# Hybrid attention and pooling layer: softmax division moved from the values' product to the split of the exponentials

## The chip, the cores and the metric

The kernel runs on one core of one Trainium2 chip. The metric is device time in microseconds (us), measured for whole executions; lower is better. One execution was also taken with the hardware profiler, and all rows below come from that one.

## The reference

One decoder layer over 1024 tokens of width 1024. A normalised input is projected to six pieces by one matrix; four of them go through causal average pooling or through attention over a sliding window of 128 tokens (8 heads of 64, 2 key/value heads, a position bias and a sink value for each head); both results are gated, projected out and added to the input.

```python
h = rmsnorm(x, norm_pre)
pool_u, pool_gate, q, k, v, attn_gate = split(h @ w_in)
pool_out = pool_mixer(pool_u, pool_w, pool_scale) * silu(pool_gate)
# attention, for each block of 128 queries, over its own and the previous block of keys
scores = q @ k.T * HEAD_DIM ** -0.5 + bias
probs = softmax(concat([scores, sink]))[..., :-1]
attn_out = (probs @ v) * silu(attn_gate)
y = concat([pool_out, attn_out]) @ w_out
x = x + rmsnorm(y, norm_post)
```

What matters here is `probs`: an exponential divided by the sum of its row, one sum for each query and head.

## The kernel before

All matrix products run in half precision, with each operand split into a high and a low part of 16 bits; three products (high by high, high by low, low by high) make up one of full precision. ScalarE writes a high part (a scaled copy), VectorE the low part (what the copy lost).

The program is written in one order by hand, and each engine executes its own instructions in that order. After a prologue, the body is a loop over **slots** `s` from 5 to 33: a slot is the projection of one group of 128 output columns for one half of the tokens (`proj`, 24 matmuls of 128x512 into the tile `acc`, of which there are two, so that a slot can start only when the result of the slot two before it has been read out by `land_slot`). At half a slot, `proj` calls `middle()`, which puts small matmuls between the two groups of 12: `spread` (the tile of that name, a transposition by which the largest weight is found; `amall`, `wp`, `ws`, `wu` on VectorE and the split of the next weights `whl` follow from it) and, late in the loop, the pooling products (`mixed`).

Attention is woven into these slots, two for each block `n` of 128 queries, an even one (s = 5 + 2n) and an odd one (s = 6 + 2n). Even slot: `score_mm(n)` on TensorE, `score_land(n)` on VectorE (bias, mask, row maximum `negm`), `exps(n)` on ScalarE: eight exponentials, one for each head, that also give the eight sums `sums`. Odd slot: `turn(n)` on ScalarE (high part of the exponentials, tile `ph`), `turn_low(n)` on VectorE (low part), then a DMA transposes `ph` into `full`. Next even slot: `mask(n)` on GpSimd makes two masked copies (`own`, `full`). Next odd slot: `pv_mm(n)` on TensorE multiplies by the values, into the one tile of `ps_pv`.

The division by the sums comes at the end of this. `turn_low` takes the reciprocals and has GpSimd spread them over a tile `r` of 128x512; `divide(n)`, called in `middle()` of the next even slot, has TensorE transpose `r` in four matmuls into the tile `rb`, which shares its place in PSUM with the values' product `pvo`, and ScalarE reads `rb` out into `cat`. Later `pv_land(n)` on VectorE multiplies the values' product by what `divide` left in `cat`.

Where pooling starts (slots 18 to 25), `land_u` on ScalarE writes the strip `ug` (and its end, `tails`), `pool_windows` on VectorE turns it into `res` one slot later, and `pool_mm` on TensorE uses `res` one slot after that. In slots 20 to 23 ScalarE also applies Silu to one quarter of the gates in `cat`, for which it loads another table once.

Of the kernel before, what the change touches and what calls it, by code (L numbers as in the profile page):

```python
# [9 lines left out]
F32 = mybir.dt.float32  # L10
# [3 lines left out]
AF = mybir.ActivationFunctionType  # L14
ALU = mybir.AluOpType
# [4 lines left out]
P = 128  # L20
# [3 lines left out]
NB = S // P  # L24
HD = 64
# [10 lines left out]
def trunk(ctx: ExitStack, tc, x, w_in, pool_w, pool_scale, attn_sinks, w_out, norm_pre, norm_post, out):  # L36
    nc = tc.nc
# [10 lines left out]
    t2 = ctx.enter_context(tc.tile_pool(name="t2", bufs=8))  # L48
# [4 lines left out]
    ps_pv = ctx.enter_context(tc.tile_pool(name="ps_pv", bufs=1, space=PSUM))  # L53
# [11 lines left out]
    def block_of(n):  # L65
        return slice(n * P, (n + 1) * P)
# [88 lines left out]
    ident = const.tile([P, P], F32, name="ident")  # L155
# [5 lines left out]
    cat = big.tile([P, KT, S], F32, name="cat")  # L161
# [59 lines left out]
    def low_w(ch):  # L221
        w, s = whl[ch], halves.pop(ch)
        nc.vector.scalar_tensor_tensor(  # L223
            w[:, 1], raws.pop(ch), s, w[:, 0], op0=ALU.mult, op1=ALU.subtract
        )
# [78 lines left out]
    vo = const.tile([P, 1], F32, name="vo")  # L304
# [41 lines left out]
    att_sc, att_s, att_p, att_f, att_r, att_o = {}, {}, {}, {}, {}, {}  # L346
# [3 lines left out]
    def score_mm(n):  # L350
        k0 = 0 if n else 1
        for pr in range(2):
            banks = [bank("sc").rearrange("p (c b s) -> p c b s", c=2, b=2) for _ in range(2)]
            for ci in range(2):
                for i, (a, b) in enumerate(PASSES):
                    for kv in range(2):
                        rows = slice(kv * HD, (kv + 1) * HD)
                        nc.tensor.matmul(  # L358
                            banks[kv][:, ci, k0:, :],
                            qT[rows, a, 2 * pr + ci, block_of(n)],  # L360
                            kT[rows, b, (n - 1 + k0) * P : (n + 1) * P],
                            start=i == 0, stop=i == 2,
                        )
            att_sc[n, pr] = banks
# [29 lines left out]
    def turn(n):  # L394
        st, sums = att_s.pop(n)
        ph = att.tile([P, 2, 8, P], F16, tag="ph", name="ph")
        nc.scalar.activation(ph[:, 0], st[:, :, :P], AF.Copy, scale=4096.0)  # L397
        att_f[n] = (st, sums, ph)

    def turn_low(n):  # L400
        st, sums, ph = att_f[n]
        nc.vector.scalar_tensor_tensor(  # L402
            ph[:, 1], st[:, :, :P], 4096.0, ph[:, 0], op0=ALU.mult, op1=ALU.subtract
        )
        full = att.tile([P, 2, 8, P], F16, tag="full", name="full", bufs=2)
        nc.sync.dma_start_transpose(
            full.rearrange("p a j t -> p (a j) t"), ph.rearrange("p a j s -> p (a j s)")
        )
        nc.vector.reciprocal(sums, sums)  # L409
        r = t2.tile([P, 512], F32, tag="t2", name="r")  # L410
        nc.gpsimd.tensor_copy(  # L411
            r.rearrange("p (c kv d) -> p c kv d", c=4, kv=2),
            sums.rearrange("p (kv c) -> p c kv", kv=2).unsqueeze(3).broadcast_to([P, 4, 2, HD]),
        )
        att_f[n] = full
        att_r[n] = r

    def mask(n):
        full = att_f.pop(n)
        if n == 0:  # L420
            att_p[n] = [(0, full)]
            return
        own = att.tile([P, 2, 8, P], F16, tag="own", name="own")
        f, o = (t.rearrange("p a j t -> p (a j) t") for t in (full, own))
        nc.gpsimd.affine_select(  # L425
            o, f, pattern=[[0, 16], [1, P]], compare_op=ALU.is_ge, fill=0.0,
            base=0, channel_multiplier=-1,
        )
        nc.gpsimd.affine_select(  # L429
            f, f, pattern=[[0, 16], [-1, P]], compare_op=ALU.is_ge, fill=0.0,  # L430
            base=-1, channel_multiplier=1,
        )
        att_p[n] = [(n, own), (n - 1, full)]


    def divide(n):
        r = att_r.pop(n)
        rb = ps_pv.tile([P, 512], F32, tag="pv", name="rb")
        for c in range(4):
            nc.tensor.transpose(rb[:, block_of(c)], r[:, block_of(c)], ident)  # L440
        nc.scalar.activation(
            cat[:, 4:8, block_of(n)], rb.rearrange("p (c t) -> p c t", t=P), AF.Copy, scale=vo
        )

    def pv_mm(n):
        parts = att_p.pop(n)
        pv = ps_pv.tile([P, 512], F32, tag="pv", name="pvo")
        total = 3 * len(parts)
        i = 0
        for tt, t in parts:  # L450
            for a, b in PASSES:
                for kv in range(2):
                    nc.tensor.matmul(  # L453
                        pv[kv * HD : (kv + 1) * HD, :],
                        vst[:, a, tt, kv * HD : (kv + 1) * HD], t[:, b, 4 * kv : 4 * kv + 4, :],
                        start=i == 0, stop=i == total - 1,
                    )
                i += 1
        att_o[n] = pv

    def pv_land(n):
        dst, pv = cat[:, 4:8, block_of(n)], att_o.pop(n)
        nc.vector.tensor_tensor(dst, pv.rearrange("p (c t) -> p c t", t=P), dst, op=ALU.mult)


    tails = const.tile([P, 4, PAD], F32, name="tails")
# [176 lines left out]
    with tc.manual_schedule(engines={ENG.PE, ENG.Activation, ENG.DVE, ENG.Pool, ENG.SP}):  # L643
# [136 lines left out]
        for s in range(5, last):  # L780
            ch, half = slots[s]
            n, odd = (s - 5) // 2, (s - 5) % 2
            if not odd:
                if 2 <= n <= NB + 1:
                    pv_land(n - 2)
                if 1 <= n <= NB:
                    mask(n - 1)
                if n < NB:
                    score_mm(n)
            elif n < NB:  # L790
                turn(n)
            if 20 <= s < 24:
                gate = cat[:, s - 20, :]
                nc.scalar.activation(gate, gate, AF.Silu)
            gates = list(pool_out)
            for key in list(pool_in):
                pool_windows(*key)

            for c2 in list(halves):
                low_w(c2)  # L800
                load_next()
            for _ in range((1, 1, 1, 0, 0, 2, 2, 2, 2, 2, 2)[s - 23] if s >= 23 else 0):
                if wo_lo < wo_hi:
                    low_wo(wo_lo)
                    wo_lo += 1


            def middle():
                for key in list(bounds):
                    if key[0] in ("wo", "c"):  # L810
                        spreads[key] = spread(bounds.pop(key))
                        if key[0] == "c":
                            scale_cat(key[1])
                        else:
                            pow2_of(widest(spreads.pop(key)), wop, wos, 14)
                            state["wo"] = True
                    elif first_slot[key] == s + 3:
                        spread_w((key,))
                        scale_w((key,))
                        high_w(key)  # L820
                if not odd and 1 <= n <= NB:
                    divide(n - 1)
                for key in gates:
                    pool_mm(*key)

            acc = proj(ch, half, middle)
            if odd and 1 <= n <= NB:
                pv_mm(n - 1)
            if odd and n < NB:
                turn_low(n)  # L830

            for c2 in order:
                if first_slot[c2] == s + 5:
                    bound_w(c2)

            if 9 <= s < 9 + KT:
                wo_raw["b", s - 9] = load_wo(s - 9)
            if 11 <= s < 11 + KT:
                bound_wo(s - 11)
            if s == 11 + KT:  # L840
                m = bounds["wo", 0] = col("wom")
                nc.vector.tensor_reduce(m, wom, axis=AX.X, op=ALU.max)
            if s >= 30:
                bound_cat(s - 30)
            if s >= 23 and wo_hi < KT:
                split_wo(wo_hi)
                wo_hi += 1
            if not odd and n < NB:
                score_land(n)
            for key in gates:  # L850
                pool_gate(*key)
            land_slot(ch, half, acc)
            if not odd and n < NB:
                exps(n)
            if s == 5 + 2 * NB + 1:
                open_late()
            if 21 <= s < 21 + KT:
                wo_raw["o", s - 21] = load_wo(s - 21)
            if s >= last - 2:
                load_res(s - last + 2)  # L860
# [47 lines left out]
```

## Time and profile before

| | |
|---|---|
| median of three executions | 346.24 us (345.97 to 347.31) |
| the profiled execution | 346.77 us, of which 345.1 us lie between its first and last instruction |
| TensorE, matmuls | 323.6 us busy, 94% of the span |
| VectorE | 199.1 us, 58% |
| ScalarE | 168.9 us, 49% |
| GpSimd | 66.2 us, 19% |
| granted TensorE clock, mean | 0.989 of full speed |

The shares are means over the whole span. A busy share says which engine has most work; whether a stretch is set by that engine is seen from the timeline, by who waits for whom there. In rows, PE is TensorE, DVE is VectorE, ACT is ScalarE, POOL is GpSimd, and L with a number is a line of the kernel before.

### The profile page before, as it was taken

How to read it: one execution, taken by the hardware profiler on the slowest of the kernel's cores; microseconds unless marked ns; L12 is line 12 of the kernel's file. 1: busy time of each engine (PE TensorE's matmuls, PEld its weight loads, DVE VectorE, ACT ScalarE, POOL GpSimd, SP SyncE). 2: the span in 40 equal slices, each digit the busy share in tenths (PEclk: the TensorE clock that was granted, in tenths of full speed). 3: DMA queues.
4: the chain of work that ended last, by engine and by line, in shares of the span. 5: the costliest groups of instructions: out<-in, count | busy, mean ns of one | idle time of the engine just before them, and what ended most of it. 6: DMA issues, size and time to landing. Idle time of an engine off the chain costs nothing.

```text
span 345.1 us, 5054 instructions
## 1 busy us (share of the span) xinstructions
PE 323.6 (94%) x1913; PEld 166.4 (48%) x1913; DVE 199.1 (58%) x423; ACT 168.9 (49%) x368; POOL 66.2 (19%) x73
## 2 busy tenths in 40 slices
PE   4689999999999999999979998799999999999993
PEld 2588556545444445445434443344444444444442
DVE  4976771537697445796979567793563633410222
ACT  4966831275656685878484443354463433211011
POOL 1100303000132344050423000000000333212330
PEclk9969999999999999999999999999999999999999
DMA  7986240001437367395240892010000241233111
GB/s 280 255 230 159 86 123 0 2 19 44 122 122 208 120 164 179 66 181 126 62 122 0 291 245 76 0 63 0 0 2 0 68 150 59 90 123 122 61 63 61
DMA packets 52090, 35.73 MB, mean 104 GB/s; under 512 B 35041, under 2 KB 45793, under 8 KB 52066
## 3 DMA queue, kind: packets, MB, share of 16 engines
q1 hardware_dynamic: 52064, 35.40, 37.1%
q8 instruction: 15, 0.25, 0.3%
q14 instruction: 9, 0.07, 0.1%
q10 hardware_dynamic: 2, 0.00, 0.0%
HBM read 27.01 MB, written 4.19 MB: 90 GB/s over the span
## 4 chain that ended last, share of the span: by engine, by line
PE 46%; DVE 19%; issue 16%; ACT 9%; POOL 6%; DMA 2%; POOLq 0%; DVEq 0%; SPq 0%; ACTq 0%
PE acc L290 30%; POOL o L639 5%; ACT st L387 4%; PE pv L272 3%; PE y L272 3%; DVE whl L223 3%; DVE st L375 2%; PE tp L250 2%; DVE win L489 2%; PE acc L272 2%; PE sc L358 2%; DVE sc L374 2%; DVE o L636 2%; PE pvo L453 1%; DVE negm L380 1%
## 5 line engine op out<-in xcount | busy, mean ns | idle before, releaser
L290 PE MATMUL acc<-hT,whl 128*128 128x512 f16 x792 | 176.7, 379 | 1.1 <-ACT gt L529 1.1
L290 PEld LDWEIGHTS <-whl 128*128 128x128 f16 x792 | 76.6, 98 | 93.9 <-issue 8.3
L272 PE MATMUL y<-wo,chl 128*128 128x512 f16 (+2 forms) x408 | 83.6, 366 | 0.0
L272 PEld LDWEIGHTS <-chl 128*128 128x128 f16 x408 | 39.0, 98 | 43.5
L219 ACT ACTIVATE whl<-wraw,ws 128x1024 f16<-128x1024 f32 x18 | 20.4, 1148 | 34.6 <-DVE wu L213 22.4
L609 ACT ACTIVATE junk<-y 128x512 bf16<-128x512 f32 (+2 forms) x17 | 9.7, 572 | 54.9 <-PE y L272 54.9
L387 ACT ACTIVATE st<-st,negm 128x129 f32<-128x129 f32 x64 | 24.8, 390 | 12.6 <-DVE negm L380 9.6
L611 DVE SCALAR_TENSOR_TENSOR eps_of<-yss,eps_of 128x1 f32<-128x1 f32 x17 | 3.2, 185 | 45.9 <-ACT junk L609 45.9
L631 POOL TENSOR_TENSOR yf<-eps_of,mhalf 128x1 f32<-128x1 f32 x7 | 3.9, 551 | 119.2 <-DVE eps_of L611 119.2
L223 DVE SCALAR_TENSOR_TENSOR whl<-wraw,ws,whl 128x1024 f16<-128x1024 f32 x18 | 23.7, 1327 | 0.0
L402 DVE SCALAR_TENSOR_TENSOR ph<-st,ph 128x1024 f16<-128x1024 f32 x8 | 9.8, 1226 | 21.6 <-ACT ph L397 21.6
L91 ACT ACTIVATE whl<-wraw 128x1024 bf16<-128x1024 f32 x18 | 18.8, 1049 | 1.5 <-DMA wraw<-in_w_in_dram 1.5
L639 POOL TENSOR_TENSOR o<-o,xr 128x512 f32<-128x512 f32 x14 | 17.5, 1269 | 9.1 <-DVE o L636 9.1
L425 POOL TENSOR_SCALAR_AFFINE_SELECT own<-full 128x2048 f16<-128x2048 f16 x7 | 14.5, 2071 | 22.9 <-DMA full<-ph 22.9
L411 POOL COPY r<-sums 128x512 f32<-128x512 f32 x8 | 4.9, 612 | 67.7 <-DVE sums L409 45.8
L250 PE MATMUL tp<-ident,h 128*128 128x128 f32 x64 | 10.9, 331 | 6.6 <-DVE h L241 3.4
L95 DVE SCALAR_TENSOR_TENSOR chl<-cat,cs,chl 128x1024 f16<-128x1024 f32 x8 | 10.3, 1284 | 10.2 <-ACT chl L94 10.2
L94 ACT ACTIVATE chl<-cat,cs 128x1024 f16<-128x1024 f32 x8 | 9.2, 1148 | 13.7 <-DVE cs L77 13.7
L375 DVE SCALAR_TENSOR_TENSOR st<-sc,qu,bias 128x256 f32<-128x256 f32 x32 | 15.2, 484 | 1.0
L429 POOL TENSOR_SCALAR_AFFINE_SELECT full<-full 128x2048 f16<-128x2048 f16 x7 | 14.4, 2055 | 0.5
L250 PEld LDWEIGHTS tp<-ident,h 128*128 128x128 f32 x64 | 9.1, 172 | 7.9 <-DVE h L241 3.8
L358 PE MATMUL sc<-kT,qT 64*128 64x256 f16 (+1 forms) x192 | 11.6, 263 | 0.6 <-DVE qT L95 0.4
(109 smaller groups left out, 371.9 us busy)
## 6 DMA issues: line engine op xcount, KB each, us to landing
wraw<-in_w_in_dram SPq DMA_DIRECT2D x10, 512.0 KB, 5.1
x<-in_x_dram SPq DMA_DIRECT2D x8, 512.0 KB, 5.4
wraw<-in_w_in_dram SPq DMA_DIRECT2D x16, 256.0 KB, 4.6
woraw<-in_w_out_dram SPq DMA_DIRECT2D x8, 512.0 KB, 5.5
woraw<-in_w_out_dram SPq DMA_DIRECT2D x16, 256.0 KB, 6.8
xr<-in_x_dram SPq DMA_DIRECT2D x8, 512.0 KB, 3.7
out_dram<-o SPq DMA_DIRECT2D x16, 256.0 KB, 2.0
post<-in_norm_post_dram SPq DMA_DIRECT2D x1, 512.0 KB, 4.2
```

The costliest lines, as they stand in the source:

```text
L91: nc.scalar.activation(junk, src, AF.Abs, accum_out=m)
L219: nc.scalar.activation(whl[ch][:, 0], raws[ch], AF.Copy, scale=halves[ch])
L223: nc.vector.scalar_tensor_tensor(w[:, 1], raws.pop(ch), s, w[:, 0], op0=ALU.mult, op1=ALU.subtract)
L250: nc.tensor.transpose(flips[tt][b][:, block_of(i)], h[:, block_of(4 * b + i)], ident)
L272: nc.tensor.matmul(acc, a, b, start=i == 0, stop=i == len(pairs) - 1)
L290: nc.tensor.matmul(acc, w[:, a, k, :], hT[:, b, k, half_of(half)], start=k == 0 and i == 0, stop=k == KT - 1 and i == 2,)
L358: nc.tensor.matmul(banks[kv][:, ci, k0:, :], qT[rows, a, 2 * pr + ci, block_of(n)], kT[rows, b, (n - 1 + k0) * P : (n + 1) * P], start=i = ...
L375: nc.vector.scalar_tensor_tensor(st[:, hs, :P], sc[:, :, 0 if n else 1, :], qu[:, 2 * pr : 2 * pr + 1], (bias if n else bias0)[:, hs, :], ...
L387: nc.scalar.activation(st[:, h, :], st[:, h, :], AF.Exp, bias=negm[:, h : h + 1], accum_out=sums[:, h : h + 1],)
L425: nc.gpsimd.affine_select(o, f, pattern=[[0, 16], [1, P]], compare_op=ALU.is_ge, fill=0.0, base=0, channel_multiplier=-1,)
L429: nc.gpsimd.affine_select(f, f, pattern=[[0, 16], [-1, P]], compare_op=ALU.is_ge, fill=0.0, base=-1, channel_multiplier=1,)
L639: nc.gpsimd.tensor_tensor(o[:, hs], o[:, hs], xr[:, hs], op=ALU.add)
```

## The change

Three things are changed. First, `turn(n)` takes the reciprocals (after a factor of 2^-12 that replaces the constant scale 4096), and the copy that made all eight heads' high part becomes eight copies of 128x128, each scaled by its head's reciprocal; `turn_low` likewise becomes eight instructions. Second, the tile `r`, its spreading by GpSimd and the whole of `divide` (four matmuls into `rb` and their readout) go, and `pv_land` reads the values' product out on ScalarE instead of multiplying on VectorE. Third, `turn(n)` is called later in its odd slot: behind the Silu of the gates, `pool_windows` and `low_w`.

```diff
     def turn(n):
         st, sums = att_s.pop(n)
         ph = att.tile([P, 2, 8, P], F16, tag="ph", name="ph")
-        nc.scalar.activation(ph[:, 0], st[:, :, :P], AF.Copy, scale=4096.0)
+        nc.vector.tensor_scalar(sums, sums, 2.0**-12, None, op0=ALU.mult)
+        nc.vector.reciprocal(sums, sums)
+        for h in range(8):
+            nc.scalar.activation(
+                ph[:, 0, h], st[:, h, :P], AF.Copy, scale=sums[:, h : h + 1]
+            )
         att_f[n] = (st, sums, ph)
     def turn_low(n):
         st, sums, ph = att_f[n]
-        nc.vector.scalar_tensor_tensor(
-            ph[:, 1], st[:, :, :P], 4096.0, ph[:, 0], op0=ALU.mult, op1=ALU.subtract
-        )
+        for h in range(8):
+            nc.vector.scalar_tensor_tensor(
+                ph[:, 1, h], st[:, h, :P], sums[:, h : h + 1], ph[:, 0, h],
+                op0=ALU.mult, op1=ALU.subtract,
+            )
...
-        nc.vector.reciprocal(sums, sums)
-        r = t2.tile([P, 512], F32, tag="t2", name="r")
-        nc.gpsimd.tensor_copy(
-            r.rearrange("p (c kv d) -> p c kv d", c=4, kv=2),
-            sums.rearrange("p (kv c) -> p c kv", kv=2).unsqueeze(3).broadcast_to([P, 4, 2, HD]),
-        )
         att_f[n] = full
-        att_r[n] = r
...
-    def divide(n):
-        r = att_r.pop(n)
-        rb = ps_pv.tile([P, 512], F32, tag="pv", name="rb")
-        for c in range(4):
-            nc.tensor.transpose(rb[:, block_of(c)], r[:, block_of(c)], ident)
-        nc.scalar.activation(
-            cat[:, 4:8, block_of(n)], rb.rearrange("p (c t) -> p c t", t=P), AF.Copy, scale=vo
-        )
...
     def pv_land(n):
-        dst, pv = cat[:, 4:8, block_of(n)], att_o.pop(n)
-        nc.vector.tensor_tensor(dst, pv.rearrange("p (c t) -> p c t", t=P), dst, op=ALU.mult)
+        nc.scalar.activation(
+            cat[:, 4:8, block_of(n)], att_o.pop(n).rearrange("p (c t) -> p c t", t=P),
+            AF.Copy, scale=vo,
+        )
...
-            elif n < NB:
-                turn(n)
             if 20 <= s < 24:
                 gate = cat[:, s - 20, :]
                 nc.scalar.activation(gate, gate, AF.Silu)
...
+            if odd and n < NB:
+                turn(n)
...
-                if not odd and 1 <= n <= NB:
-                    divide(n - 1)
                 for key in gates:
                     pool_mm(*key)
```

What stands on VectorE in odd slot 18 (block 6) and at the start of slot 19, before: the low weights, the row of small steps after `spread`, the low part of all heads (L402), the reciprocals (L409), and then `pv_land` of block 5 (L463) ahead of the pooling windows.

```order
L380 TENSOR_REDUCE negm<-st 128x8
L223 SCALAR_TENSOR_TENSOR whl<-wraw,ws,whl 128x1024
L87 TENSOR_REDUCE amall<-spread 128x1
...
L213 TENSOR_TENSOR wu<-wp,gsc 128x1
L402 SCALAR_TENSOR_TENSOR ph<-st,ph 128x1024
L409 RECIPROCAL sums<-sums 128x8
L478 MEMSET ug 128x16
L463 TENSOR_TENSOR cat<-pvo,cat 128x4x128
L489 TENSOR_TENSOR win<-ug 128x527
```

The same place after:

```order
L380 TENSOR_REDUCE negm<-st 128x8
L223 SCALAR_TENSOR_TENSOR whl<-wraw,ws,whl 128x1024
L397 TENSOR_SCALAR sums<-sums 128x8
L398 RECIPROCAL sums<-sums 128x8
L87 TENSOR_REDUCE amall<-spread 128x1
...
L213 TENSOR_TENSOR wu<-wp,gsc 128x1
L408 SCALAR_TENSOR_TENSOR ph<-st,sums,ph 128x128 x8
L470 MEMSET ug 128x16
L481 TENSOR_TENSOR win<-ug 128x527
```

The reciprocals now stand ahead of the small steps, where they wait for the sums, and `pv_land` is gone from VectorE.

On ScalarE from block 6's exponentials to the landing of slot 20 (L474, `ug`), before:

```order
L387 ACTIVATE st,sums<-st,negm 128x129 x8
L397 ACTIVATE ph<-st 128x1024
L219 ACTIVATE whl<-wraw,ws 128x1024
L91 ACTIVATE junk,wom<-woraw 128x1024
L474 ACTIVATE ug<-acc,wu 128x512
...
L387 ACTIVATE st,sums<-st,negm 128x129 x8
L397 ACTIVATE ph<-st 128x1024
L794 ACT_TABLE_LOAD
L794 ACTIVATE cat<-cat 128x1024
L474 ACTIVATE ug<-acc,wu 128x512
```

The same after:

```order
L387 ACTIVATE st,sums<-st,negm 128x129 x8
L400 ACTIVATE ph<-st,sums 128x128 x8
L219 ACTIVATE whl<-wraw,ws 128x1024
L91 ACTIVATE junk,wom<-woraw 128x1024
L466 ACTIVATE ug<-acc,wu 128x512
...
L387 ACTIVATE st,sums<-st,negm 128x129 x8
L784 ACT_TABLE_LOAD
L784 ACTIVATE cat<-cat 128x1024
L400 ACTIVATE ph<-st,sums 128x128 x8
L466 ACTIVATE ug<-acc,wu 128x512
```

In each block one copy has become eight ahead of the next landing, and in block 7 the table load and the Silu stand ahead of them.

## Rows read from the trace of the kernel before

**Rows 1.** Page, busy time of an engine, share of the span, instructions
```profile
PE 323.6 (94%) x1913; PEld 166.4 (48%) x1913; DVE 199.1 (58%) x423; ACT 168.9 (49%) x368; POOL 66.2 (19%) x73
```

**Rows 2.** Groups by line and shape: count, busy us, mean ns of one, idle before
```profile
L440 PE MATMUL rb<-ident,r 128*128 128x128 f32 x32 | 4.9, 276 | 2.8 <-DVE cat L463 2.6 <-POOL r L411 0.2
...
L463 DVE TENSOR_TENSOR cat<-pvo,cat 128x512 f32<-128x512 f32 x8 | 5.3, 665 | 0.3 <-PE pvo L453 0.3
...
L397 ACT ACTIVATE ph<-st 128x1024 f16<-128x1024 f32 x8 | 8.5, 1057 | 0.3
...
L402 DVE SCALAR_TENSOR_TENSOR ph<-st,ph 128x1024 f16<-128x1024 f32 x8 | 9.8, 1226 | 21.6 <-ACT ph L397 21.6
...
L387 ACT ACTIVATE st<-st,negm 128x129 f32<-128x129 f32 x64 | 24.8, 390 | 12.6 <-DVE negm L380 9.6 <-DVE ug L478 3.0
...
L219 ACT ACTIVATE whl<-wraw,ws 128x1024 f16<-128x1024 f32 x18 | 20.4, 1148 | 34.6 <-DVE wu L213 22.4 <-DVE ws L77 12.2
...
L95 DVE SCALAR_TENSOR_TENSOR vst<-pv,vst 128x128 f16<-128x128 f32 x8 | 2.1, 289 | 11.6 <-ACT vst L94 11.6
```

**Rows 3.** Timeline of TensorE, slot 7's middle: start us, us, engine, line, idle before
```profile
78.89 0.60 PE L440 MATMUL rb<-ident,r 128*128 128x128 f32 x4
...
79.33 5.34 PE L290 MATMUL acc<-hT,whl 128*128 128x512 f16 x24
```

**Rows 4.** Timeline, blocks 1 to 5, VectorE, ScalarE and TensorE
```profile
91.69 0.69 DVE L95 SCALAR_TENSOR_TENSOR qT<-acc,qT 128x512 f16<-128x512 f32 x1 [1.22 <-ACT qT L94]
...
106.11 0.67 ACT L524 ACTIVATE cat<-acc,wu 128x512 f32<-128x512 f32 x1
...
107.83 7.93 PE L290 MATMUL acc<-hT,whl 128*128 128x512 f16 x36
...
135.17 0.29 DVE L87 TENSOR_REDUCE amall<-spread 128x1 f32<-128x128 f32 x1 [3.52 <-PE spread L82]
```

**Rows 5.** Timeline of ScalarE and VectorE, from block 6's exponentials to slot 20's landing
```profile
157.91 0.19 ACT L387 ACTIVATION_READ_ACCUMULATOR st<-st,negm 128x1 f32 x1
...
159.09 1.14 ACT L219 ACTIVATE whl<-wraw,ws 128x1024 f16<-128x1024 f32 x1
...
160.13 1.04 ACT L91 ACTIVATE junk<-woraw 128x1024 bf16<-128x1024 f32 x1
...
161.92 0.71 DVE L489 TENSOR_TENSOR win<-ug 128x527 f32<-128x527 f32 x1 [0.76 <-ACT ug L474]
...
164.93 0.16 DVE L369 COPY st<-sinks 128x8 f32<-128x8 f32 x1
...
172.87 0.19 ACT L387 ACTIVATION_READ_ACCUMULATOR st<-st,negm 128x1 f32 x1
...
176.42 0.67 ACT L474 ACTIVATE ug<-acc,wu 128x512 f32<-128x512 f32 x1
...
176.99 0.27 ACT L479 ACTIVATE tails<-acc,wu 128x16 f32<-128x16 f32 x1
```

**Rows 6.** Timeline, slots 21 to 28, VectorE, GpSimd, ScalarE and TensorE
```profile
176.54 0.75 DVE L511 SCALAR_TENSOR_TENSOR cat<-mixed,pscale,cat 128x512 f32<-128x512 f32 x1 [1.03 <-ACT cat L794]
...
179.40 2.46 POOL L425 TENSOR_SCALAR_AFFINE_SELECT own<-full 128x2048 f16<-128x2048 f16 x1 [3.12 <-DMA full<-ph]
...
180.03 2.37 DVE L495 SCALAR_TENSOR_TENSOR res<-win,ug 128x512 f32<-128x512 f32 x1
...
182.44 1.85 DVE L500 TENSOR_TENSOR win<-win,invc 128x7 f32<-128x7 f32 x1
...
192.52 0.29 DVE L87 TENSOR_REDUCE amall<-spread 128x1 f32<-128x128 f32 x1 [0.54 <-PE spread L82]
...
193.48 1.15 ACT L219 ACTIVATE whl<-wraw,ws 128x1024 f16<-128x1024 f32 x1 [3.40 <-DVE wu L213]
...
212.32 0.32 PE L82 MATMUL spread<-ident,as 128*128 128x128 f32 x1 [1.50 <-DVE amall L87]
...
224.34 9.01 PE L290 MATMUL acc<-hT,whl 128*128 128x512 f16 x41 [1.11 <-ACT gt L529]
```

## The prediction

> **What bounds the kernel now.** I read the page first: TensorE is busy nearly all of the span [rows 1], so work taken from TensorE looks like time won. The groups by line say how much there is: `divide` is 32 small matmuls with 2.8 us of idle time in front of them [rows 2]. Then I read the timeline block by block, because a mean share hides who is late. Call E the end of a block's exponentials, with all eight sums read out: 158.10 for block 6, 173.06 for block 7 (start plus length of the last accumulator read) [rows 5]. From E to E runs a serial loop that TensorE isn't in: copy (ScalarE), low part (VectorE), the other VectorE work in order, scores, maximum, exponentials. The reader should look for who waits for whom. Around block 5 VectorE waits 3.52 us for TensorE's `spread` [rows 4]: there TensorE sets the pace. Around block 6 VectorE waits for ScalarE's `ug` [rows 5]. From slot 23 on ScalarE waits for VectorE's `wu`, and TensorE itself stands still for VectorE (1.50 us) and ScalarE (1.11 us) [rows 6]: from 192.5 to 224.3 the loop of VectorE and ScalarE sets the pace and TensorE follows. Up to there, then, what counts is when VectorE comes to `amall` of slot 23, at 192.52. Time that TensorE saves earlier is worth something only if that moves.
>
> **The change, part by part.**
>
> *TensorE.* From the first `rb` matmul to the next projection matmul it is 79.33 - 78.89 = 0.44 us [rows 3]; eight times makes 3.5, and with the 2.8 idle [rows 2] at most 6.3 us. GpSimd's spreading of `r` goes too; nothing but `rb` waits for it, so I count nothing for it.
>
> *ScalarE's copies.* No row has a copy of 128 columns with a pointer scale. An exponential of 129 columns with a pointer bias takes 390 ns, a copy of 1024 with a pointer scale 1148 [rows 2]: 758 ns for 895 columns, 0.85 each, so 389 ns for 128. Neighbours overlap: L219 runs 1.14 and its follower starts 1.04 later [rows 5], 0.10 less. Eight make 7 x 0.29 + 0.39 = 2.4 us, where one copy took 1.06 [rows 2]. Bounds: without the pointer's part (1148 - 1057 = 91 ns [rows 2]) the pitch is 0.20 and the sum 1.7; without overlap it is 3.1. I take 2.4, since the exponentials are the nearest row in size and have a pointer.
>
> *The new round trip.* The copies wait for two VectorE steps of eight columns, which wait for E. Nearest: from `amall` at 192.52 to L219 at 193.48 five small steps pass, 0.19 each [rows 6]; two make 0.4. So ScalarE's next instruction, which began 0.99 after E (159.09), begins 0.4 + 2.4 - 0.1 = 2.7 after it: **1.7 us later in each block** (bounds 1.0 and 2.5). Queued behind it are the high weights, the maxima and the landing of the slot's `acc`, and for that landing TensorE waits two slots later.
>
> *VectorE's low parts.* One of 128 columns out of PSUM takes 289 ns [rows 2]; I take 0.35 with the pointer and an SBUF source. They follow the copies head by head, so only the last one adds: they end 0.4 + 2.4 + 0.4 = 3.2 after E, where before it was 1.06 + 1.23 and two hand-overs, 2.35. Against that, `pv_land`'s 0.67 [rows 2] no longer stands behind them: VectorE's own chain grows by 0.2 a block. `pv_land` on ScalarE replaces the readout of `rb`, one for one, in time that ScalarE spent waiting.
>
> [...]
>
> *Where the delays meet, blocks 1 to 5.* For the first blocks VectorE waits on ScalarE's landing of q (1.22 [rows 4]); 1.7 more there, less `pv_land`, puts E of block 2 about 1.1 to 1.4 later, and the landing of slot 10 (106.11 + 0.67 [rows 4]) 3 us later, at about 109.8. Slot 12 wants that buffer; it began at 107.83 + 12 x 0.216 = 110.4 (36 matmuls in 7.93 [rows 4]), and TensorE, ahead by three `rb` and their idle time, would be there at 108.2. So TensorE waits again, some 1.6 us, for a landing in place of `rb`: what it saved there is spent. VectorE's lag in turn ends in its 3.52 us wait at 135.17 [rows 4]. I take both engines there as before within 0.5.
>
> *Blocks 6 and 7.* E of block 6 stays within 0.2. Then `ug` lands 1.7 later, VectorE already waits for it (L489 at 161.92, 0.76 idle [rows 5]), so the windows start at 163.6, the scores of block 7 (164.93) at 166.6, and E of block 7 goes from 173.06 to 174.75. After it come table load, Silu, copies, landing of slot 20. The reciprocals are ready under the table load; the copies take 1.36 more than the one copy. The landing ended at 176.99 + 0.27, 4.2 after E [rows 5]; now 5.56 after, 180.3. The last copy ends as the landing begins, 179.55, the last low part at 179.9 (before 173.06 + 2.35 = 175.4).
>
> *VectorE from there to `amall`.* Before, 192.52 - 175.4 = 17.1 us. Off come two `pv_land` (1.33), the wait for the Silu (1.03 in front of L511) and for `spread` (0.54) [rows 6], since both are early now. In the rest lie two stretches blocked by GpSimd's masks of block 7: L495 took 2.37 where the like L489 takes 0.71, and L500 1.85 for seven columns where L369 takes 0.16 for eight [rows 5, 6]: 3.35 us. Without them 10.85 are left: `amall` at 190.8; with all of them 194.1. The masks start 4.0 after the low parts (179.40 - 175.4), so now at 183.9. By then VectorE has done L511, three sums, `res` and two small steps (0.75 + 4 x 0.72 + 0.35) and reaches 183.9 too. The masks then fall on the four window sums of the next strip: about 1.3 lost to each of two masks, 2.6. `amall` at 193.4: **0.9 us later**. TensorE's `spread` is not later: the masks end by about 188.6, then half of block 7's product (0.7) and half a slot (2.6), 191.9.
>
> *The sum.* From 193.4 on all is as before, so the end moves by 0.9: the profiled execution would take 346.77 + 0.9 = 347.7. It lies 0.5 above the median, so I predict 346.24 + 0.9 = **347.1**. Of 6.3 us saved on TensorE nothing arrives. With the bounds: copies at 1.7 take 0.7 off E of block 7 and 0.7 off the copies (345.7); no blocked stretch takes 2.6 off (344.5); copies at 3.1 add 1.5, the full block 0.7 (349.3). The likeliest case's own range is 344.5 to 349.3.
>
> **The rivals.**
>
> *TensorE's saving arrives.* For it: 94% busy [rows 1], and the wait of 3.52 at block 5. Then 346.24 - 6.3 = 339.9. Against it: E to E has no TensorE work in it at blocks 6 and 7. In part, with the short pitch and fewer blocked stretches, it gives 342 to 344.4. Both together 0.17.
>
> *The loop becomes the bound in every block (slower).* If the copies take 3.1, VectorE's chain grows by about 0.9 a block rather than 0.2: E of block 6 is 0.9 late, `ug` another 2.5, so E of block 7 is 3.4 late; with copies 0.7 longer the low parts end at 182.3, and `amall` comes 13.5 later at 195.8: +3.3, 349.5. It decides once the copies take over 2.9 us, when the added lag of blocks 5 and 6 no longer hides. For it: ScalarE's waits are short there. Against it: the overlap of 0.10. 0.20.
>
> *The masks block the strip before, not the next one.* The two finish within 0.1 us of each other in my working. L500 and L495 show what a mask costs VectorE [rows 6]. If a mask starts first, the last small step ends 2 us later, TensorE's `mixed` and slot 22 with it, `spread` of slot 23 at 194.0, `amall` at 194.3: +1.8, 348.0. 0.13. [...]
>
> **How the numbers follow.** A difference under 0.5% (1.7 us) is about what a measurement of this kernel can't tell from none. The forecast has 0.50 and lies inside it, gain cases 0.17, loop-bound 0.20, masks 0.13, which ends on the border. So faster 0.17, same 0.50, slower 0.33. The range reaches from 344.5 to 350.0: it leaves out the gain cases at the low end and little above.
>
> **What would show it.** `rb` gone and TensorE less busy by 3.5 to 5 us, with its idle time grown as much. Eight copies of about 0.39 at a pitch of 0.29. A wait of TensorE at slot 12 or 22 for ScalarE's landing. E of block 5 within 0.5 of before, E of block 7 about 1.7 later, `amall` of slot 23 near 193.4, and the same 31 us from there to TensorE's start of slot 28. I am wrong if the copies' pitch is 0.2 or 0.39, if E of block 7 isn't later, or if VectorE's stretch from the low parts to `amall` isn't about 13.5.

## The result and the profile after

The changed kernel takes 349.01 us (median of 4 runs, 348.55 to 349.47), the kernel before 346.22 on the same chip (345.97 to 347.31): ratio 1.008, interval 1.0064 to 1.0095. It is slower by 2.8 us, 0.8%. The time lies in the predicted range, but 1.9 us above the predicted 347.1 and beyond the 0.5% within which the prediction had put its likeliest case; it had given "slower" a chance of 0.33.

TensorE did get the work taken off. This is the page's row of engines (busy time, share of the span, instructions), to be held against [rows 1]:

```profile
PE 320.3 (92%) x1881; PEld 163.1 (47%) x1881; DVE 204.5 (59%) x479; ACT 179.4 (52%) x424; POOL 61.3 (18%) x65
```

TensorE is busy 3.3 us less in a span that is 2.0 us longer. The groups by line and shape (count, busy us, mean ns of one, idle before) show the new instructions:

```profile
L400 ACT ACTIVATE ph<-st,sums 128x128 f16<-128x128 f32 x64 | 19.5, 388 | 4.0 <-ACT st L387 3.4 <-DVE sums L398 0.5
L408 DVE SCALAR_TENSOR_TENSOR ph<-st,sums,ph 128x128 f16<-128x128 f32 x64 | 18.4, 350 | 3.4 <-ACT ph L400 3.4
...
L452 ACT ACTIVATE cat<-pvo,vo 128x512 f32<-128x512 f32 x8 | 5.4, 672 | 0.6 <-PE pvo L443 0.6
```

A copy takes 388 ns and a low part 350 ns, where 389 and 350 were expected. So what came on top of the forecast was not lost on the price of an instruction. It was lost where they stand. The timeline of ScalarE, VectorE and GpSimd from the end of block 6's exponentials to `amall` of slot 23 (start us, us, engine, line, idle before), to be held against [rows 5, 6]:

```profile
157.37 0.18 ACT L387 ACTIVATION_READ_ACCUMULATOR st<-st,negm 128x1 f32 x1
...
157.58 0.17 DVE L397 TENSOR_SCALAR sums<-sums 128x8 f32<-128x8 f32 x1 [1.75 <-ACT st L387]
...
158.08 2.45 ACT L400 ACTIVATE ph<-st,sums 128x128 f16<-128x128 f32 x8 [0.53 <-ACT st L387]
158.70 2.21 DVE L408 SCALAR_TENSOR_TENSOR ph<-st,sums,ph 128x128 f16<-128x128 f32 x8
160.43 1.13 ACT L219 ACTIVATE whl<-wraw,ws 128x1024 f16<-128x1024 f32 x1
...
163.21 0.71 DVE L481 TENSOR_TENSOR win<-ug 128x527 f32<-128x527 f32 x1 [2.27 <-ACT ug L466]
...
164.95 1.28 DVE L223 SCALAR_TENSOR_TENSOR whl<-wraw,ws,whl 128x1024 f16<-128x1024 f32 x1
165.75 2.34 POOL L425 TENSOR_SCALAR_AFFINE_SELECT own<-full 128x2048 f16<-128x2048 f16 x1 [11.00 <-DMA full<-ph]
166.21 1.91 DVE L369 COPY st<-sinks 128x8 f32<-128x8 f32 x1
168.03 0.42 DVE L374 COPY_PREDICATED sc<-own_key,sc 128x256 f32<-128x256 uint16 x1
168.16 2.00 POOL L429 TENSOR_SCALAR_AFFINE_SELECT full<-full 128x2048 f16<-128x2048 f16 x1
168.48 0.49 DVE L375 SCALAR_TENSOR_TENSOR st<-sc,qu,bias 128x256 f32<-128x256 f32 x1
...
175.84 0.19 ACT L387 ACTIVATION_READ_ACCUMULATOR st<-st,negm 128x1 f32 x1
...
178.72 2.39 DVE L408 SCALAR_TENSOR_TENSOR ph<-st,sums,ph 128x128 f16<-128x128 f32 x8 [1.52 <-ACT ph L400]
...
185.06 2.02 POOL L425 TENSOR_SCALAR_AFFINE_SELECT own<-full 128x2048 f16<-128x2048 f16 x1 [14.90 <-DMA full<-ph]
186.00 1.64 DVE L481 TENSOR_TENSOR win<-ug 128x527 f32<-128x527 f32 x1
187.68 3.85 DVE L481 TENSOR_TENSOR win<-win 128x525 f32<-128x525 f32 x3
...
194.59 0.28 DVE L87 TENSOR_REDUCE amall<-spread 128x1 f32<-128x128 f32 x1
```

The row to look at is 166.21: a copy of eight columns takes 1.91 us, where the same copy took 0.16 before [rows 5]. GpSimd's mask of block 6 began 0.46 us ahead of it, and the copy ends as the mask ends. Before, the copy (164.93 [rows 5]) stood 0.95 us ahead of that mask (timeline of GpSimd, kernel before):

```profile
165.88 2.01 POOL L425 TENSOR_SCALAR_AFFINE_SELECT own<-full 128x2048 f16<-128x2048 f16 x1 [4.59 <-DMA full<-ph]
```

Behind the copy stand the scores, the maximum and the exponentials of block 7, so E of block 7 is late by as much.

On TensorE the saved time has turned into waits: the span less its busy time grew from 21.5 to 26.8 us. Some of them (timeline of TensorE, kernel after):

```profile
108.89 5.34 PE L290 MATMUL acc<-hT,whl 128*128 128x512 f16 x24 [1.87 <-ACT cat L516]
...
181.51 2.75 PE L290 MATMUL acc<-hT,whl 128*128 128x512 f16 x12 [1.20 <-ACT tails L471]
...
214.39 0.32 PE L82 MATMUL spread<-ident,as 128*128 128x128 f32 x1 [2.79 <-DVE amall L87]
...
226.41 3.83 PE L290 MATMUL acc<-hT,whl 128*128 128x512 f16 x17 [1.11 <-ACT gt L521]
```

From `amall` of slot 23 to TensorE's start of slot 28 it is 226.41 - 194.59 = 31.8 us, as before [rows 6].

**How the profiled executions are compared.** The start of a program differs by up to 1.7 us between executions: E of block 0 lies at 73.37 before, at 72.31 after, and from 72.44 to 73.99 in the experiments. So I cut each span into four lengths, from E of block 0 to the last instruction. Their sum, set against that of the kernel before, agrees with the difference of the medians within 0.6 us in every kernel.

| kernel | us, median (range) | ratio to before [interval] | E0 to E6 | E6 to E7 | E7 to `amall` of slot 23 | from there to the end | sum |
|---|---|---|---|---|---|---|---|
| before | 346.22 (345.97 to 347.31) | | 84.7 | 15.0 | 19.5 | 152.6 | 271.7 |
| after | 349.01 (348.55 to 349.47) | 1.0080 [1.0064, 1.0095] | 85.2 | 18.5 | 18.6 | 152.5 | 274.8 |
| e1 no division, one copy | 343.68 (343.19 to 344.10) | 0.9918 [0.9901, 0.9935] | 81.8 | 16.6 | 18.1 | 152.5 | 269.0 |
| e2 sinks by ScalarE | 349.71 (349.54 to 349.91) | 1.0094 [1.0078, 1.0110] | 85.1 | 18.8 | 18.6 | 152.5 | 275.0 |
| e3 `turn` at its old place | 348.44 (347.82 to 349.11) | 1.0058 [1.0042, 1.0075] | 85.2 | 16.7 | 19.2 | 152.5 | 273.7 |
| e4 before, in eight pieces | 353.82 (352.02 to 355.15) | 1.0206 [1.0179, 1.0232] | 88.2 | 16.2 | 22.3 | 152.5 | 279.2 |
| e5 `low_w` later in slot 19 | 346.96 (345.66 to 348.51) | 1.0012 [0.9996, 1.0028] | 85.2 | 15.5 | 18.6 | 152.5 | 271.8 |
| e6 the same in all blocks | 345.55 (344.76 to 348.43) | 0.9986 [0.9964, 1.0009] | 83.6 | 15.8 | 19.1 | 152.5 | 271.0 |
| e7 before, with e6's edit | 345.24 (344.75 to 346.37) | 0.9963 [0.9950, 0.9977] | 84.3 | 13.8 | 20.0 | 152.5 | 270.5 |
| e8 readout on VectorE | 352.22 (351.19 to 352.39) | 1.0155 [1.0133, 1.0177] | 85.6 | 18.5 | 21.1 | 152.6 | 277.7 |
| e9 e6, landing first | 343.29 (342.63 to 345.19) | 0.9921 [0.9898, 0.9943] | 82.7 | 14.5 | 18.6 | 152.5 | 268.4 |
| e10 e9, gates a slot later | 346.05 (345.57 to 346.90) | 0.9991 [0.9980, 1.0002] | 82.7 | 14.5 | 19.4 | 154.6 | 271.2 |
| e11 e7, landing first | 345.86 (345.23 to 346.87) | 0.9983 [0.9972, 0.9994] | 84.3 | 13.1 | 21.5 | 152.5 | 271.4 |

The length from `amall` of slot 23 to the end tests the prediction's claim that from there on all goes as before. It is 152.5 or 152.6 in every kernel but e10, whose edit lengthens that part. The loss of the change lies in E6 to E7 (+3.5), with +0.5 ahead of it and -0.9 behind.

### The profile page after: what moved, and what is told of

It reads as the page before. It is cut to its first block, busy times and chain, and to the rows that moved or that the text cites. A ratio compares the mean times of both kernels' runs of the same rounds, so it can differ in the third digit from the quotient of the medians.

```text
span 347.1 us, 5073 instructions
## 1 busy us (share of the span) xinstructions
PE 320.3 (92%) x1881; PEld 163.1 (47%) x1881; DVE 204.5 (59%) x479; ACT 179.4 (52%) x424; POOL 61.3 (18%) x65
## 5 line engine op out<-in xcount | busy, mean ns | idle before, releaser
L272 PE MATMUL y<-wo,chl 128*128 128x512 f16 (+2 forms) x408 | 83.6, 366 | 0.0
L223 DVE SCALAR_TENSOR_TENSOR whl<-wraw,ws,whl 128x1024 f16<-128x1024 f32 x18 | 23.5, 1316 | 1.4 <-ACT whl L219 1.4
L400 ACT ACTIVATE ph<-st,sums 128x128 f16<-128x128 f32 x64 | 19.5, 388 | 4.0 <-ACT st L387 3.4
L408 DVE SCALAR_TENSOR_TENSOR ph<-st,sums,ph 128x128 f16<-128x128 f32 x64 | 18.4, 350 | 3.4 <-ACT ph L400 3.4
L91 ACT ACTIVATE whl<-wraw 128x1024 bf16<-128x1024 f32 x18 | 18.8, 1049 | 1.3 <-DMA wraw<-in_w_in_dram 1.3
L250 PE MATMUL tp<-ident,h 128*128 128x128 f32 x64 | 11.7, 350 | 5.9 <-DVE h L241 3.4
L94 ACT ACTIVATE chl<-cat,cs 128x1024 f16<-128x1024 f32 x8 | 9.2, 1148 | 13.8 <-DVE cs L77 13.8
L375 DVE SCALAR_TENSOR_TENSOR st<-sc,qu,bias 128x256 f32<-128x256 f32 x32 | 15.2, 484 | 1.0
L481 DVE TENSOR_TENSOR win<-ug 128x527 f32<-128x527 f32 x8 | 6.6, 822 | 11.4 <-ACT ug L468 8.9
L250 PEld LDWEIGHTS tp<-ident,h 128*128 128x128 f32 x64 | 9.9, 182 | 7.3 <-DVE h L241 3.8
```

Of the source, the lines that this page charges most:

```text
L91: nc.scalar.activation(junk, src, AF.Abs, accum_out=m)
L223: nc.vector.scalar_tensor_tensor(w[:, 1], raws.pop(ch), s, w[:, 0], op0=ALU.mult, op1=ALU.subtract)
L250: nc.tensor.transpose(flips[tt][b][:, block_of(i)], h[:, block_of(4 * b + i)], ident)
L272: nc.tensor.matmul(acc, a, b, start=i == 0, stop=i == len(pairs) - 1)
L375: nc.vector.scalar_tensor_tensor(st[:, hs, :P], sc[:, :, 0 if n else 1, :], qu[:, 2 * pr : 2 * pr + 1], (bias if n else bias0)[:, hs, :], ...
L400: nc.scalar.activation(ph[:, 0, h], st[:, h, :P], AF.Copy, scale=sums[:, h : h + 1])
```

## The experiments

Each was measured beside the kernel before (346.57 beside e1 to e4, 346.38 beside e5 to e8, 346.52 beside e9 to e11).

**e1: no division, one copy.** The changed kernel with one copy and one low part, and no reciprocals. It leaves out the division.

```diff
-        nc.vector.tensor_scalar(sums, sums, 2.0**-12, None, op0=ALU.mult)
-        nc.vector.reciprocal(sums, sums)
-        for h in range(8):
-            nc.scalar.activation(
-                ph[:, 0, h], st[:, h, :P], AF.Copy, scale=sums[:, h : h + 1]
-            )
+        nc.scalar.activation(ph[:, 0], st[:, :, :P], AF.Copy, scale=4096.0)
...
-        for h in range(8):
...
+        nc.vector.scalar_tensor_tensor(
+            ph[:, 1], st[:, :, :P], 4096.0, ph[:, 0], op0=ALU.mult, op1=ALU.subtract
+        )
```

> The changed kernel with one unscaled copy and one low part for all eight heads and no reciprocals: it leaves out the division by the sums, everything else of the change stands (no matmuls into rb, ScalarE reads the values' product out, the copy behind the Silu). Theory loop (the added time sits in ScalarE's and VectorE's pieces, which make the exponentials of block 7 late): block 7's exponentials end about 1 us earlier than in the kernel before instead of 4 later, counted from block 0's; total 344 to 345.5. Rival tail (the place behind table load and Silu and the masks of block 7 cost the time, not the pieces): 347.5 to 349. Rival TensorE (only the pieces stood in the way of the whole saving): 340 to 341.5.

343.68, just below the first range: 2.9 less than before, 5.3 less than after (5.8 by the sums of the table). So the eight pieces with their round trip cost 5.3 to 5.8 us, and the rest of the change is worth 2.9, of the 6.3 at most that the prediction counted for TensorE. That saving comes in ahead of E of block 6 (81.8 against 84.7); near block 5 TensorE sets the pace there, for VectorE waits 4.44 us for `spread` (at 132.39). The copy of eight columns is hit here too (timeline of GpSimd and VectorE):

```profile
161.12 2.35 POOL L418 TENSOR_SCALAR_AFFINE_SELECT own<-full 128x2048 f16<-128x2048 f16 x1 [8.88 <-DMA full<-ph]
161.59 1.91 DVE L369 COPY st<-sinks 128x8 f32<-128x8 f32 x1
```

So the collision doesn't need the pieces. It needs `score_land` to come after the mask's start.

**e2: the struck copy moved to ScalarE.**

```diff
-        nc.vector.tensor_copy(st[:, :, P], sinks)
+        nc.scalar.copy(st[:, :, P], sinks)
```

> The changed kernel with one edit: the copy of the sinks into the scores' tile, eight columns, runs on ScalarE instead of VectorE. Theory loop: in block 7 that copy took 1.91 us on VectorE behind GpSimd's mask instead of 0.16, so block 7's exponentials end about 1.7 us earlier than in the changed kernel and the total falls by 1.0 to 1.8, to 347.2 to 348. Rival tail (what follows block 7's exponentials sets the end): 348.7 to 349.2, no difference.

349.71, above both ranges: nothing is won. The mask struck the neighbour instead, the low weights, which take 1.28 alone (same view):

```profile
165.31 2.02 POOL L425 TENSOR_SCALAR_AFFINE_SELECT own<-full 128x2048 f16<-128x2048 f16 x1 [10.12 <-DMA full<-ph]
165.36 3.03 DVE L223 SCALAR_TENSOR_TENSOR whl<-wraw,ws,whl 128x1024 f16<-128x1024 f32 x1
...
167.39 2.87 POOL L429 TENSOR_SCALAR_AFFINE_SELECT full<-full 128x2048 f16<-128x2048 f16 x1
```

It cost 1.75 us there, as it had on the copy. What counts is that an instruction which a mask can block stands at that time in the loop, not which one.

**e3: `turn` at its old place**, at the odd slot's start.

```diff
+            elif n < NB:
+                turn(n)
             if 20 <= s < 24:
...
-            if odd and n < NB:
-                turn(n)
```

> The changed kernel with its third part undone: turn(n) at the start of the odd slot again, so copies ahead of the Silu, but the two small VectorE steps, which wait for the sums, ahead of the pooling windows and low weights. Theory loop: VectorE waits for the sums before the low weights that it did in that time; low parts end about 1.5 us later in blocks 1, 2, 5, 6, and in block 7 the windows stand between; 350 to 352. Rival tail (copies behind table load and Silu are the cost): 347.3 to 348.2.

348.44, within 0.6 of after and not the 350 to 352 expected. E6 to E7 is 1.8 shorter, because the copy comes just ahead of the mask (timeline of VectorE and GpSimd):

```profile
167.27 0.16 DVE L369 COPY st<-sinks 128x8 f32<-128x8 f32 x1
...
167.80 2.01 POOL L425 TENSOR_SCALAR_AFFINE_SELECT own<-full 128x2048 f16<-128x2048 f16 x1 [11.16 <-PE spread L82]
```

The copy starts 8.7 us after E of block 6, as it does in after; only the mask is later. So this run shows what the block by the mask costs with VectorE at the same place: 1.8. But E7 to `amall` is 0.7 longer, and the sum only 1.1 shorter. The place of `turn` is at most a small part of the cost.

**e4: the kernel before, in eight pieces.** The scale is a constant tile, so only the pieces are added; `rb` and its readout stay.

```diff
-        nc.scalar.activation(ph[:, 0], st[:, :, :P], AF.Copy, scale=4096.0)
+        for h in range(8):
+            nc.scalar.activation(ph[:, 0, h], st[:, h, :P], AF.Copy, scale=big4[:, :1])
...
-        nc.vector.scalar_tensor_tensor(
-            ph[:, 1], st[:, :, :P], 4096.0, ph[:, 0], op0=ALU.mult, op1=ALU.subtract
-        )
+        for h in range(8):
+            nc.vector.scalar_tensor_tensor(
+                ph[:, 1, h], st[:, h, :P], big4[:, :1], ph[:, 0, h],
```

> The kernel before with one edit: eight copies and eight low parts, one for each head, with a pointer scale that holds 4096, in place of one of each; division as before. Theory loop: the pieces alone delay ScalarE by 1.36 us a block and the low parts by 0.5, so block 7's exponentials end 1.5 to 2 us later; total 348 to 350. Rival (division, new waits and moved readout cost the time, pieces are hidden): 345.8 to 347.

353.82: the pieces alone cost 7.3 us, more than expected. The order of before makes it worse: there `rb` shares its buffers with the values' product, and `pv_land` on VectorE stands behind the later low parts and behind a gate that waits 1.90 us for ScalarE's Silu (timeline of TensorE):

```profile
184.02 1.09 PE L445 MATMUL rb<-ident,r 128*128 128x128 f32 x4 [5.04 <-DVE cat L468]
```

TensorE waits 5.04 us, where it waited 1.83 for the same before and the longest wait of after in slots 21 and 22 is 1.20. Of the time lost, 3.5 us lie ahead of E of block 6; what they went into isn't shown in full (one wait for `rb` is 2.01 there, 0.76 before). So the change's three parts belong together: pieces alone +7.3, the rest alone -2.9 (e1), all of it +2.8. They don't add up (4.4 by the sum), since the rest also takes away what the pieces would delay.

**e5: the low weights out of the way in slot 19.** `low_w` (L223) goes behind `score_land`, in one slot. This brings the copy ahead of the mask.

```diff
+            late_w = list(halves)
+            if not (s == 19):
                 for c2 in late_w:
                     low_w(c2)
                     load_next()
...
                 score_land(n)
+                if s == 19:
+                    for c2 in late_w:
+                        low_w(c2)
+                        load_next()
```

> The changed kernel with one edit, in slot 19 alone: the low weights that stand on VectorE between the pooling windows and the scores of block 7 go behind the scores. The first experiments showed that taking one VectorE instruction out of the way of GpSimd's mask of block 6 only hands the wait (1.75 us) to its neighbour; now the scores, which read PSUM, should stand beside the mask. Theory loop: block 7's exponentials end 1.3 us earlier for the order and 1.7 for the wait, 3.0 in all, amall of slot 23 as much; total 346 to 347. Rival tail (masks of block 7, table load and Silu set the end, whatever block 7's exponentials do): 348.5 to 349.3.

346.96, as expected. The copy has its old length:

```profile
165.98 0.17 DVE L369 COPY st<-sinks 128x8 f32<-128x8 f32 x1
...
166.54 2.00 POOL L425 TENSOR_SCALAR_AFFINE_SELECT own<-full 128x2048 f16<-128x2048 f16 x1 [10.77 <-DMA full<-ph]
```

Counted from E of block 0, E of block 7, `amall` and the end all come 3.0 earlier than after. One instruction moved in one slot moves the whole program by what it moves E of block 7: this is the loop as the bound, shown. (The medians differ by 2.1; this kernel's runs spread over 2.9 us.)

**e6 and e7: the same edit in every block**, in the changed kernel (e6) and in the kernel before (e7); the condition is `not odd and n < NB` in place of `s == 19`.

> The changed kernel with the low weights behind the scores in every even attention slot. Theory loop: also blocks 1, 2, 5 and 6 get 1.3 us shorter from exponentials to exponentials, but what is gained up to block 5 goes into waiting for TensorE there; so only blocks 6 and 7 count, total 345 to 347. Rival tail: 348.5 to 349.3.

> The kernel before with the same edit: low weights behind the scores in every even attention slot. Theory loop: the same serial loop sets the time from block 6 on, so its two last rounds get 1.3 us shorter each: 343.5 to 345.5. Rival TensorE (the kernel before is bound by TensorE): no change, 346 to 347.

345.55 and 345.24, both as expected. Beside e5, e7 isolates the collision. In slot 19 of before no mask strikes that copy, and the edit shortens E6 to E7 by 1.2 (15.0 to 13.8); in the changed kernel the same edit in slot 19 shortens it by 3.0 (e5). The 1.8 between them is the block by the mask, as in e3. In e6 a mask found another victim, the last small step of slot 21 (0.17 alone), and TensorE waited for it:

```profile
180.77 2.00 POOL L425 TENSOR_SCALAR_AFFINE_SELECT own<-full 128x2048 f16<-128x2048 f16 x1 [12.44 <-DMA full<-ph]
180.81 1.99 DVE L493 TENSOR_TENSOR res<-win,ug 128x7 f32<-128x7 f32 x1
...
182.94 1.10 PE L498 MATMUL mixed<-res,pw 128*128 128x512 f32 x2 [2.92 <-DVE res L493]
```

That is the rival "masks block the strip before". It missed the changed kernel by 0.02 us (L493 starts at 185.04, the mask at 185.06). Counted from E of block 7, the step and the mask come at 9.03 and 8.99 here, at 9.01 and 9.03 in the changed kernel: hundredths decide which is first.

**e8: the readout back on VectorE**, in the changed kernel.

```diff
-        nc.scalar.activation(
+        nc.vector.tensor_scalar(
             cat[:, 4:8, block_of(n)], att_o.pop(n).rearrange("p (c t) -> p c t", t=P),
-            AF.Copy, scale=vo,
+            vo, None, op0=ALU.mult,
         )
```

> The changed kernel with one part undone: the values' product is read out by VectorE (a scaled copy, 0.67 us) instead of ScalarE. Theory loop: 0.67 more on VectorE in each round from exponentials to exponentials, 0.67 less on ScalarE, which waits there anyway; the rounds of blocks 6 and 7 and the stretch up to slot 23 count: 349.5 to 351.5. Rival (the readout on ScalarE delays its landings and is what costs): 347 to 348.3.

352.22, 3.2 more than after and more than expected. It goes into E7 to `amall` (21.1 against 18.6). With the readout (0.73) ahead of them, VectorE's small steps in slot 21 came behind the mask of block 7, and TensorE waited for them (timeline of GpSimd, VectorE and TensorE):

```profile
185.77 2.07 POOL L425 TENSOR_SCALAR_AFFINE_SELECT own<-full 128x2048 f16<-128x2048 f16 x1 [14.89 <-DMA full<-ph]
186.00 1.85 DVE L492 TENSOR_TENSOR win<-win,invc 128x7 f32<-128x7 f32 x1
...
188.20 1.10 PE L498 MATMUL mixed<-res,pw 128*128 128x512 f32 x2 [3.23 <-DVE res L493]
...
195.03 0.75 DVE L452 TENSOR_SCALAR cat<-pvo,vo 128x512 f32<-128x512 f32 x1 [0.54 <-PE pvo L443]
...
197.83 0.29 DVE L87 TENSOR_REDUCE amall<-spread 128x1 f32<-128x128 f32 x1 [0.70 <-PE spread L82]
```

The struck step took 0.17 in after. VectorE loses no more to the masks than there (1.68 and 0.93), but it loses the 1.68 ahead of `res`, where the prediction's third rival had it; so TensorE is late in slot 22, and VectorE waits for it in turn, 0.54 and 0.70 us. The two readouts themselves (0.73 and 0.75) are about the other half of the 2.5. So the move of the readout to ScalarE is a gain inside the change, and a good part of it is a collision avoided.

**e9: e6 with the landing first.** `bound_wo` (L91 on `woraw`, 1.04 us between the copies and `ug`) goes behind `land_slot`.

```diff
-            if 11 <= s < 11 + KT:
-                bound_wo(s - 11)
...
             land_slot(ch, half, acc)
+            if 11 <= s < 11 + KT:
+                bound_wo(s - 11)
```

> The changed kernel with low weights behind the scores, and in slots 11 to 18 ScalarE lands the slot's product ahead of the maximum of an output weight tile (1.14 us) instead of behind it. Theory loop: VectorE waits for that landing after block 6's copies, so the round from block 6's to block 7's exponentials falls from 15.8 to about 14.6 us and the total by 1.1, to 344.2 to 344.8. Rival tail (the masks of block 7 and TensorE's waits behind them set the end): 345.2 to 346, no change against the run without this edit.

343.29, the fastest kernel here, ahead of before by 3.2 (ratio 0.9921) and of after by 5.7 (1.6%; the two were not measured side by side). That is 0.9 below the expected range: E6 to E7 fell by 1.3 as expected, but E0 to E6 fell too, by 0.9, and E7 to `amall` by 0.5. Counted from E of block 6, `ug` comes 1.3 earlier (3.9 against 5.2), the copy is clear of the mask, and the wait of `mixed` falls from 2.92 (e6) to 0.56:

```profile
161.76 0.17 DVE L369 COPY st<-sinks 128x8 f32<-128x8 f32 x1
...
163.91 2.00 POOL L425 TENSOR_SCALAR_AFFINE_SELECT own<-full 128x2048 f16<-128x2048 f16 x1 [10.72 <-DMA full<-ph]
...
179.24 1.10 PE L498 MATMUL mixed<-res,pw 128*128 128x512 f32 x2 [0.56 <-DVE res L493]
```

**e10: e9 with `pool_gate` a slot later**, meant to take the last 0.56.

```diff
+            for key in gate_late:
+                pool_gate(*key)
...
-            for key in gates:
-                pool_gate(*key)
...
+            gate_late = gates
```

> As the run before, and each pool_gate (0.75 us on VectorE, out of PSUM) goes one slot later, behind that slot's pooling windows. In the earlier run with low weights behind the scores the last small window step of slot 21 met GpSimd's mask of block 7 and took 1.99 us, and TensorE waited 2.92 us for it; 0.75 earlier it should be through. Theory loop with masks: a further 0.3 to 1.5 us, 343 to 344.3. Rival: the mask only finds the next two-input instruction, no change against the run before.

346.05: a miss, worse than e9 by 2.8. E to E is as in e9 and the wait of `mixed` is down to 0.16, but the edit also put the gate (L503) ahead of `amall` in slots 23 and on, where it stood behind it. The timeline of VectorE:

```profile
189.92 0.74 DVE L503 SCALAR_TENSOR_TENSOR cat<-mixed,pscale,cat 128x512 f32<-128x512 f32 x1
190.58 0.28 DVE L87 TENSOR_REDUCE amall<-spread 128x1 f32<-128x128 f32 x1
...
200.60 0.28 DVE L87 TENSOR_REDUCE amall<-spread 128x1 f32<-128x128 f32 x1
...
208.38 0.74 DVE L503 SCALAR_TENSOR_TENSOR cat<-mixed,pscale,cat 128x512 f32<-128x512 f32 x1
...
211.43 0.28 DVE L87 TENSOR_REDUCE amall<-spread 128x1 f32<-128x128 f32 x1
```

From `amall` to `amall` it is now 10.0 and 10.8 us, in e9 9.4 and 10.1: the loop of the last slots grew by the gate's 0.7 each time. That VectorE's loop sets the pace there is seen from the other side.

**e11: e7 with the landing first**, the same edit in the kernel before.

> The kernel before with both reorderings of the two runs ahead of this one that it can have: low weights behind the scores, and ScalarE's landing ahead of the output weight maximum. Theory loop: ScalarE is less late there with one copy, VectorE waited 0.76 us for the landing of slot 18; a further 0.5 to 0.8 us against the run with low weights alone: 344.3 to 344.9. Rival TensorE: its rows are in the way, no further change, 345 to 345.6.

345.86, above both ranges: no further gain. E6 to E7 is the shortest of all (13.1), but E7 to `amall` grows to 21.5. TensorE now waits in `rb` for `pv_land`, and VectorE for `spread`:

```profile
177.02 0.63 PE L440 MATMUL rb<-ident,r 128*128 128x128 f32 x4 [1.87 <-DVE cat L463]
...
191.39 0.29 DVE L87 TENSOR_REDUCE amall<-spread 128x1 f32<-128x128 f32 x1 [0.77 <-PE spread L82]
```

With both edits in both kernels, the new division is ahead of the old one by 2.6 us (e9 against e11, measured side by side). With the first edit alone it was not (e6 345.55, e7 345.24), and against e7, the best kernel here with the old division, e9 is ahead by 2.1, each counted from the kernel before beside it.

## Why the prediction was right or wrong

**The bound: right.** The loop of ScalarE and VectorE sets the time from block 6 on, and TensorE's saving didn't arrive (e5, and the constant 152.5). TensorE was busy 3.3 us less, where 3.5 to 5 were forecast.

**The prices: right.** 388 ns a copy and eight in 2.45 us (2.4), 350 ns a low part, and the last low part of block 6 ends 158.70 + 2.21 - (157.37 + 0.18) = 3.36 after E (3.2). The 0.35 stood 0.06 above the row it started from (289 ns, out of PSUM), the author's estimate for the pointer and the SBUF source; the runs show 350 for the two together, not the share of each.

**Blocks 1 to 5: right.** TensorE's new wait at slot 12 is 1.87 (1.6), and E of block 5 stays at 71.1 after E of block 0. E of block 6 is 0.5 late where 0.2 was allowed: VectorE waits 0.69 for the high weights in slot 16, another piece of ScalarE's lag.

**Block 7: the step that failed.** "Then `ug` lands 1.7 later, VectorE already waits for it ..., so the windows start at 163.6, the scores of block 7 (164.93) at 166.6, and E of block 7 goes from 173.06 to 174.75." The first half holds: the windows start 163.21 - 157.55 = 5.66 after E of block 6, before 3.82, so 1.84 later. But the step carried VectorE's delay along without looking what GpSimd does at the new time. Before, the copy (164.93) was 0.95 ahead of the mask. Counted from E of block 0, VectorE came 2.3 later and the mask 0.9 later, so the copy stood 0.46 behind it, and lost 1.75 (e3, and e5 with e7, each show 1.8 for this block by the mask). Thus 1.84 and 1.75 together make E6 to E7 3.5 longer (18.48 against 14.96), not 1.7. The prediction's sum has no term for the mask of block 6 and gives no reason for that; this 1.75 and the 0.3 of block 6 are its error. The same kind of collision was worked out one block later, and that part was right. The two instructions at which the prediction had seen what a mask costs, L495 and L500, have two inputs; the struck copy has one.

**E7 to `amall`: right.** 18.56 against 18.65. The masks begin 3.95 after the low parts (4.0) and fall on the window sums of the next strip, which lose 0.93 and 1.68 (2.6 in all, as forecast, though shared out otherwise than 1.3 and 1.3). That they fall there and not on the small step ahead was decided by 0.02 us: in e6 a small step was struck, and in e8 too. So it is in part luck that the right strip was named.

**The rivals.** TensorE's saving arrives only in part and only where nothing else is later (e1). The loop as bound in every block, with copies of 3.1, is not what happened, though its +3.3 is close to the measured +3.1: the copies took 2.45, and blocks 1 to 5 hide their lag. The masks did add a loss, but it was the mask of block 6, ahead of E of block 7, not a mask of block 7 in the strip named. That 349.0 lies inside the range is luck: the room above 347.1 was made for copies of 3.1 us and a fully blocked strip, and neither came; the block in slot 19 filled it.

## What to carry to other kernels

In this kernel a delay on one engine had to be carried not only along its own queue but against every other engine that can hold it up at the new time, as the mask did here. A collision that the trace avoids by less than a microsecond is a price that a small shift can switch on: 0.95 us of room was lost in slot 19, and 0.02 decided the strip of slot 21. And an engine that is busy 94% is not the bound where it stands in no part of the loop that ends last: here the edit that relieves it paid only after that loop had been shortened at two places (e9 against e11), not at one (e6 against e7).

## What the runs showed of the hardware

A mask of GpSimd held up even a one-source fp32 copy of eight columns in SBUF: L369 took 1.91 us beside the first mask of block 6, where it took 0.16 before, 1.75 more. VectorE's instructions with an operand in PSUM ran beside the second mask at the length that they have in the whole of the kernel after: L374 0.42 (median of 28: 0.419), L375 0.49 and 0.48 (median of 32: 0.485). What it is in the copy that lets a mask hold it up, no run shows. Where the low weights (L223) met a mask, the one that started second took longer, and that could be GpSimd's: L223 behind the first mask of e2 took 3.03 (1.28 at 164.95 in after) and that mask 2.02, while the masks that started when L223 was still running took 2.34 (after), 2.35 (e1) and 2.87 (the second of e2), where the second mask of block 6 took 2.00 in after.
